# One distance between moving operand and weights: four operand buffers of a split-precision decoder trunk, on one Trainium2 core

## The chip, the cores and the metric

The kernel is one program on one core of a Trainium2 chip. The metric is its device time in microseconds (us), the median of several runs. Five engines are named as in the profile: PE (TensorE, with its weight loads as PEld), DVE (VectorE), ACT (ScalarE), POOL (GpSimd) and SP (SyncE, which issues most of the transfers).

## The reference

One decoder layer on 16 meta tokens and 256 tokens of width 2048, all in float32. What matters here is its chain of products:

```
xn   = rmsnorm(h)
proj = xn @ w_in                                  # attention and linear-attention inputs, gates
y    = sigmoid(gate_fox) * (o_fox @ w_o_fox) + sigmoid(gate_gla) * (o_gla @ w_o_gla)
h    = h + y @ w_out
h    = h + square(relu(rmsnorm(h) @ w_ff1)) @ w_ff2       # 2048 -> 8192 -> 2048
out  = rmsnorm(h)[:, 16:]
```

The heads of the two token mixers lie between `proj` and `y`; the change does not touch them.

## The kernel before, in words

Activations are kept transposed: 128 channels of a block on the 128 partitions, tokens along the free dimension. A matrix of 2048 columns of input is therefore 16 blocks, numbered k, and one *weight chunk* is a 2048 x 128 piece of a weight matrix: 16 blocks of 128 x 128. The order of the chunks is a list (`stream`), and the products follow it.

Each float32 factor is split in two: an upper part *hi*, rounded to the format in which PE takes it in one pass, and a lower part *lo*, the rest. A weight chunk arrives by two transfers of 512 KB on SP's queue (line 122); ACT writes hi (line 124) and DVE writes lo = raw - hi (line 125), side by side in one of five weight buffers `wt`, in half chunks of 8 blocks: hi of a block is 512 bytes per partition, lo of the same block the 512 bytes behind it. A product leaves out lo times lo. So `gemm2` (line 143) runs 16 *pairs* per chunk, with a moving operand of 256 tokens whose row k holds its own hi and lo next to each other:

```
        nc.tensor.matmul(ps, hi, x, start=first, stop=False)                          # L140: 512 columns
        nc.tensor.matmul(ps[:, 0:NT], lo, x[:, 0, :], start=False, stop=last)         # L141: 256 columns
```

A *row* of an operand is thus 2 x 256 numbers of 4 bytes, 2048 bytes per partition. The operands of `gemm2`:

- `x` (normalised input, rows of 272 tokens, so 2176 bytes) and `of` (attention output, 8 rows): not touched by the change.
- `og` (output of linear attention) and `x2` (normalised input of the MLP) share one buffer, "s2". The profile leaves buffer numbers out, so `x2` is printed as `x` there.
- `y` (input of `w_out`) and `a` (output of the first MLP matrix, a group of 2048 of the 8192 channels at a time, so four times) share another buffer, "s1".

`operand` (line 225) takes a tile of S1 or S2 numbers and cuts the 16 rows out of it at places given as a list. Before, `steps` (line 236) gives row k the place first + 512 k + (0, 64, 128 or 192) numbers for the four quarters of the rows: rows 2048 bytes apart, and 256 bytes more at every fourth. `first` is another one for each operand (lines 239 to 242).

From the token mixers on, the chunks run so: 8 rounds of four gate chunks on `x`, one on `of` (two halves of 8 pairs) and two on `og` (16 chunks of `og` in all); 16 chunks on `y` (line 789 and behind: each result is added to `h`, and `x2`'s row is made of it); then four times 16 chunks on `x2` followed by 16 chunks on `a`. In the last group only 12 chunks of `a` run as pairs; the last four keep their upper weights (`whi_last`, in buffer "s2") and run lo for all tokens first (line 850), then hi for 128 tokens at a time (line 859), so that the end can be normalised and stored in halves. In the MLP every product of the first matrix goes through `relu2` (lines 815 to 820), and every product of the second through `add_residual` (lines 774 to 777), on ACT and DVE. The instructions of an engine are put in order by a scheduler when the program is built.

Of the kernel before, what the change touches and what calls it, by code (L numbers as in the profile page):

```python
# [18 lines left out]
KT = D // P  # L19
NM = 16  # L20
NT = 256
# [44 lines left out]
def trunk(ctx: ExitStack, tc: tile.TileContext, hT, w_small, w_all, consts, w_alpha2, out):  # L66
# [3 lines left out]
    def nm(s):  # L70
        serial[0] += 1
        return f"{s}_{serial[0]}"

    const = ctx.enter_context(tc.tile_pool(name="const", bufs=1))
    keep = ctx.enter_context(tc.tile_pool(name="keep", bufs=1))
# [53 lines left out]
    def next_weights(keep_hi=None):  # L129
        c = chunk[0]  # L130
        chunk[0] += 1
        parts = []
        for i in range(2):
            hi, lo, step = weight_half(c, i, None if keep_hi is None else keep_hi[:, HK * i : HK * (i + 1), :])
            step(0, HK)
            parts.append((hi, lo))
        return lambda k: (parts[k // HK][0][:, k % HK, :], parts[k // HK][1][:, k % HK, :])
# [5 lines left out]
    def gemm2(w, x, k0=0, nk=KT):  # L143

        ps = bank(pg, "ps")
        for k in range(nk):
            hi, lo = w(k0 + k)
            mac2(ps, hi, lo, x[k], k == 0, k == nk - 1)
        issued()
        return ps  # L150
# [74 lines left out]
    def operand(pool, name, size, places, tag):  # L225


        t = pool.tile([P, size], F32R, tag=tag, name=nm(name))
        rows = []
        for at, gap in places:  # L230
            both = t[:, at : at + 2 * gap].rearrange("p (o t) -> p o t", t=gap) if at + 2 * gap <= size else None
            rows.append(both[:, :, 0:NT])
        return rows

    S1, S2 = 8728, 8628
    def steps(first, *by):
        return [(first + 512 * k + by[k * len(by) // KT], NT) for k in range(KT)]

    AT_OG = steps(8, 0, 64, 128, 192)
    AT_Y = steps(48, 0, 64, 128, 192)  # L240
    AT_X2 = steps(40, 0, 64, 128, 192)
    AT_A = [steps(e, 0, 64, 128, 192) for e in (16, 40, 12, 58)]


    h = keep.tile([P, KT, NA + 3], F32, name="h")
# [23 lines left out]
    def gain(i, k):  # L269
        return h[:, k, NA + i : NA + i + 1]  # L270
# [55 lines left out]
    for s in range(KT // 2):  # L326
# [3 lines left out]
        for kk in range(2):  # L330
            k = 2 * s + kk
# [100 lines left out]
    og_box = []  # L432

    def og_tile():
        if not og_box:
            og_box.append(operand(keep, "og", S2, AT_OG, "s2"))
        return og_box[0]

    def gla_gates(ts):
# [20 lines left out]
    def gla_head(hd, sg, ready=None):  # L460
# [122 lines left out]
        def scale():  # L583
            pr = st["pr"]
            spread(pr, st["y"], (0, P), NT)
            nc.scalar.copy(rg, pr[:, 0:NT])
            for i in range(4):
                j = 4 * hd + i
                nc.vector.scalar_tensor_tensor(oT[:, i, :], oT[:, i, :], ggn[:, j : j + 1], rg, op0=ALU.mult,
                                               op1=ALU.mult)  # L590
                nc.vector.tensor_tensor(oT[:, i, :], oT[:, i, :], st["sg"][:, i, :], op=ALU.mult)
                split_to(og_tile()[j][:, 0, :], og_tile()[j][:, 1, :], oT[:, i, :])
# [34 lines left out]
    for hd in range(1, GLA_H):  # L627
        gla_head(hd, None)
    flush()
    og = og_tile()  # L630


# [112 lines left out]
    for j0 in range(0, KT, 2):  # L745
# [5 lines left out]
        for j in range(2):  # L751
            t = total(gemm2(next_weights(), og))
            nc.vector.tensor_tensor(t, gates[2 * j + 1], t, op=ALU.mult)
            nc.vector.tensor_tensor(yf[:, j0 + j, :], gates[2 * j], t, op=ALU.add)
    y = operand(keep, "y", S1, AT_Y, "s1")
    for j in range(KT):
        split_to(y[j][:, 0, :], y[j][:, 1, :], yf[:, j, :])
    mix.close()
# [1 line left out]


    ht = h[:, :, NM:NA]
    x2 = operand(keep, "x2", S2, AT_X2, "s2")

    def square_sum(j, acc):
        if j == 0:
            nc.scalar.activation(acc, ht[:, j, :], AF.Square)
        else:
            sq = gat.tile([P, NT], F32, tag="hsq", name=nm("hsq"))
            nc.scalar.activation(sq, ht[:, j, :], AF.Square)  # L770
            nc.gpsimd.tensor_tensor(acc, acc, sq, op=ALU.add)

    def add_residual(j, ps):
        b = tmp.tile([P, NT], F32, tag="evb", name=nm("evb"))
        nc.scalar.copy(b, ps[:, NT:512])  # L775
        nc.vector.tensor_tensor(ht[:, j, :], ps[:, 0:NT], ht[:, j, :], op=ALU.add)
        nc.vector.tensor_tensor(ht[:, j, :], ht[:, j, :], b, op=ALU.add)
# [37 lines left out]
    def relu2(a, f, ps):  # L815
        t = total(ps)
        nc.vector.scalar_tensor_tensor(t, t, 0.0, r2b, op0=ALU.max, op1=ALU.mult)
        s = gat.tile([P, NT], F32, tag="asq", name=nm("asq"))
        nc.vector.tensor_tensor(s, t, t, op=ALU.mult)
        split_to(a[f][:, 0, :], a[f][:, 1, :], s)  # L820

    acc = gat.tile([P, NT], F32, tag="acc", name="acc3", bufs=1)
    for g in range(NG):
        a = operand(keep, "a", S1, AT_A[g], "s1")
        held = []
        for f in range(KT):
            ps = gemm2(next_weights(), x2)
            if g == 0 and f == 0:
                held.append(ps)
                continue  # L830
            if g == 0 and f == 1:
                relu2(a, 0, held.pop())
            relu2(a, f, ps)
        last = g == NG - 1
        for j in range(KT - NL if last else KT):
            add_residual(j, gemm2(next_weights(), a))
            if last:
                square_sum(j, acc)
                nc.scalar.activation(ht[:, j, :], ht[:, j, :], AF.Identity, scale=gain(2, j))
                if j == 0:  # L840
                    tc.keep_in_program_order(nc.scalar.preload_act_table_set("sqrt_and_others"))
# [121 lines left out]
```

## Time and profile before

| what | value |
|---|---|
| device time, median of 3 runs | 1631.77 us (1631.02 to 1631.82) |
| profiled execution, its own time | 1631.39 us |
| profiled execution, its span (first to last instruction) | 1629.7 us |
| PE busy | 1612.4 us, 99% |
| DVE, ACT, POOL busy | 1048.0, 793.7, 91.2 us |
| granted PE clock, mean | 0.996 |
| DMA | 292.97 MB, mean 180 GB/s |

The span lies within the profiled execution's own time, 1.7 us short of it. PE's busy time includes the overlap of matmuls in its pipeline: how long a matmul really takes of PE is read from the start of one to the start of the next, not from its listed duration.

### The profile page before, as it was taken

Reading aid. Unit: us, or ns where it says so; the run is one execution under the profiler, and the core shown is the slowest. Engines: PE = TensorE matmul, PEld = TensorE weight load, DVE = VectorE, ACT = ScalarE, POOL = GpSimd, SP = SyncE. Lnnn points to the kernel's source line nnn. Section 1 sums busy time; section 2 is a strip of 40 time slices with the busy share of each in tenths; the row PEclk is TensorE's granted clock in tenths of the full one; section 3 lists DMA queues with packets and bytes.
Section 4 is the critical chain, followed back from the end, with each engine's and each line's share of the span. In section 5 each row is a group of like instructions: output and inputs, shape, how many; then the busy total and the mean of one; then the engine's idle time right before and its main releaser. Section 6 shows DMA issues by size and latency. Waiting matters only on the chain.

```text
span 1629.7 us, 25555 instructions
## 1 busy us (share of the span) xinstructions
PE 1612.4 (99%) x9996; PEld 1450.3 (89%) x9996; DVE 1048.0 (64%) x1591; ACT 793.7 (49%) x1217; POOL 91.2 (6%) x144
## 2 busy tenths in 40 slices
PE   8999999999999999999999999999999999999997
PEld 7999999999998888888888888888888888888886
DVE  6766757476556566665677776567656776667655
ACT  6555444454445444444565444444444444444563
POOL 0100000010000000000011000000000000000012
PEclk9999999999999999999999999999999999999998
DMA  8444555454455555555555555555555555555552
GB/s 290 156 143 156 165 161 165 157 195 157 157 161 173 184 191 190 187 191 189 188 189 189 183 190 182 190 186 190 178 197 193 184 188 188 191 184 190 185 193 66
DMA packets 90265, 292.97 MB, mean 180 GB/s; under 512 B 9096, under 2 KB 21648, under 8 KB 89888
## 3 DMA queue, kind: packets, MB, share of 16 engines
q1 hardware_dynamic: 87552, 288.88, 54.1%
q8 instruction: 79, 1.29, 0.3%
q10 hardware_dynamic: 2416, 1.33, 0.3%
q0 software_dynamic: 176, 1.12, 0.2%
q14 instruction: 42, 0.34, 0.1%
HBM read 289.19 MB, written 2.11 MB: 179 GB/s over the span
## 4 chain that ended last, share of the span: by engine, by line
PE 98%; DMA 1%; DVE 0%; ACT 0%; issue 0%; SPq 0%; DVEq 0%; ACTq 0%
PE ps L140 50%; PE ps L141 26%; PE psa L159 5%; PE psa L158 5%; PE psa L157 5%; PE ps L345 1%; PE ps L859 1%; DMA h<-hT_dram 1%; PE pa L506 1%; PE ps L850 0%; PE ps L352 0%; PE po L570 0%; DMA raw<-w_all_dram 0%; PE pz L404 0%; ACT x L332 0%; PE po L571 0%
## 5 line engine op out<-in xcount | busy, mean ns | idle before, releaser
L125 DVE TENSOR_TENSOR wt<-raw,wt 128x1024 fp32r<-128x1024 f32 x522 | 644.7, 1235 | 330.0 <-ACT wt L124 320.0
L124 ACT CAST wt<-raw 128x1024 fp32r<-128x1024 f32 x522 | 548.7, 1052 | 397.3 <-issue 158.6
L140 PE MATMUL ps<-x,wt 128*128 128x512 f32 x1952 | 688.4, 395 | 0.0
L141 PE MATMUL ps<-x,wt 128*128 128x256 f32 x1952 | 551.3, 282 | 0.0
L140 PEld LDWEIGHTS ps<-x,wt 128*128 128x128 f32 x1952 | 366.8, 188 | 83.1
L141 PEld LDWEIGHTS ps<-x,wt 128*128 128x128 f32 x1952 | 367.9, 188 | 0.0
L140 PE MATMUL ps<-a,wt 128*128 128x512 f32 x960 | 336.8, 394 | 0.0
L141 PE MATMUL ps<-a,wt 128*128 128x256 f32 x960 | 270.8, 282 | 0.0
L140 PEld LDWEIGHTS ps<-a,wt 128*128 128x128 f32 x960 | 180.7, 188 | 41.0
L157 PE MATMUL psa<-x,wt 128*128 128x272 f32 x640 | 187.3, 293 | 0.0
L159 PE MATMUL psa<-x,wt 128*128 128x272 f32 x640 | 184.8, 289 | 0.0
L158 PE MATMUL psa<-x,wt 128*128 128x272 f32 x640 | 184.4, 288 | 0.0
L141 PEld LDWEIGHTS ps<-a,wt 128*128 128x128 f32 x960 | 181.5, 189 | 0.0
L166 ACT COPY evb<-ps 128x256 f32<-128x256 f32 x160 | 59.3, 373 | 237.6 <-PE ps L141 235.4
L169 DVE TENSOR_TENSOR evt<-ps,evb 128x256 f32<-128x256 f32 x158 | 66.9, 424 | 107.1 <-ACT evb L166 106.9
L157 PEld LDWEIGHTS psa<-x,wt 128*128 128x128 f32 x640 | 120.3, 188 | 0.7
L158 PEld LDWEIGHTS psa<-x,wt 128*128 128x128 f32 x640 | 120.4, 188 | 0.2
L159 PEld LDWEIGHTS psa<-x,wt 128*128 128x128 f32 x640 | 120.4, 188 | 0.1
L140 PE MATMUL ps<-y,wt 128*128 128x512 f32 x256 | 89.4, 393 | 0.0
L140 PE MATMUL ps<-og,wt 128*128 128x512 f32 x256 | 89.1, 394 | 0.0
L775 ACT COPY evb<-ps 128x256 f32<-128x256 f32 x76 | 28.3, 372 | 113.0 <-PE ps L141 112.9
L141 PE MATMUL ps<-y,wt 128*128 128x256 f32 x256 | 71.7, 280 | 0.0
(261 smaller groups left out, 1396.1 us busy)
## 6 DMA issues: line engine op xcount, KB each, us to landing
raw<-w_all_dram SPq DMA_DIRECT2D x537, 512.0 KB, 3.9
raw<-w_all_dram SPq DMA_DIRECT2D x7, 384.0 KB, 6.8
h<-hT_dram SPq DMA_DIRECT2D x1, 1100.0 KB, 10.0
negc<-fdram POOLq DMA_DIRECT2D x1, 1088.0 KB, 6.0
out_dram<-h SPq DMA_DIRECT2D x3, 256.0 KB, 2.6
out_dram<-h ACTq DMA_DIRECT2D x3, 256.0 KB, 3.1
h<-hT_dram SPq DMA_DIRECT2D x1, 550.0 KB, 7.3
raw<-w_all_dram SPq DMA_DIRECT2D x2, 256.0 KB, 4.4
```

Of the source, the lines that this page charges most:

```text
L124: nc.scalar.copy(hi[:, k, :], r)
L125: nc.vector.tensor_tensor(lo[:, k, :], r, hi[:, k, :].bitcast(F32), op=ALU.subtract)
L140: nc.tensor.matmul(ps, hi, x, start=first, stop=False)
L141: nc.tensor.matmul(ps[:, 0:NT], lo, x[:, 0, :], start=False, stop=last)
L157: nc.tensor.matmul(ps[:, 0:n], hi, x[:, k, 0, :], start=(k == 0), stop=False)
L158: nc.tensor.matmul(ps[:, 0:n], lo, x[:, k, 0, :], start=False, stop=False)
L159: nc.tensor.matmul(ps[:, 0:n], hi, x[:, k, 1, :], start=False, stop=(k == KT - 1))
L166: nc.scalar.copy(b, ps[:, NT:512])
L169: nc.vector.tensor_tensor(t, ps[:, 0:NT], b, op=ALU.add)
L345: nc.tensor.matmul(ps, hi, x[:, k, :, NM:NA], start=st, stop=False)
L506: nc.tensor.matmul(dst, k[:, a, :], q[:, a, :], start=(a == 0), stop=(a == 1))
L775: nc.scalar.copy(b, ps[:, NT:512])
```

## The change

Every row of `og`, `y`, `x2` and `a` is put at the same place modulo 256 bytes, and the extra 256 bytes at each fourth row go: rows are exactly 2048 bytes apart. Buffer "s2" becomes 384 numbers (1536 bytes) shorter.

```
-    S1, S2 = 8728, 8628
-    def steps(first, *by):
-        return [(first + 512 * k + by[k * len(by) // KT], NT) for k in range(KT)]
-
-    AT_OG = steps(8, 0, 64, 128, 192)
-    AT_Y = steps(48, 0, 64, 128, 192)
-    AT_X2 = steps(40, 0, 64, 128, 192)
-    AT_A = [steps(e, 0, 64, 128, 192) for e in (16, 40, 12, 58)]
+    S1, S2 = 8728, 8244
+    AT_S1 = [(40 + 512 * k, NT) for k in range(KT)]
+    AT_S2 = [(16 + 512 * k, NT) for k in range(KT)]
...
-            og_box.append(operand(keep, "og", S2, AT_OG, "s2"))
+            og_box.append(operand(keep, "og", S2, AT_S2, "s2"))
...
-    y = operand(keep, "y", S1, AT_Y, "s1")
+    y = operand(keep, "y", S1, AT_S1, "s1")
...
-    x2 = operand(keep, "x2", S2, AT_X2, "s2")
+    x2 = operand(keep, "x2", S2, AT_S2, "s2")
...
-        a = operand(keep, "a", S1, AT_A[g], "s1")
+        a = operand(keep, "a", S1, AT_S1, "s1")
```

The addresses that the built programs give (bytes from a partition's start): "s1" begins at 36928 and "s2" at 71840 in both. The five weight buffers begin at 127936 and every 8192 behind it before, and at 126400 and every 8192 behind it after: all that lies behind "s2" moves down by 1536 bytes, a multiple of 512. So hi and lo of every block begin at 192 modulo 256 in both programs. The table gives the *distance*: where a row of the operand begins, minus where its weights begin, modulo 256 bytes.

| operand | pairs | distance before | distance after |
|---|---|---|---|
| `x` | 928 | 192 and 64 in turn | the same |
| `of` | 128 | 0 | the same |
| `og` | 256 | 0 | 32 |
| `y` | 256 | 64 | 32 |
| `x2` | 1024 | 128 | 32 |
| `a`, group 0 | 256 | 192 | 32 |
| `a`, group 1 | 256 | 32 | 32 |
| `a`, group 2 | 256 | 176 | 32 |
| `a`, group 3 | 192 | 104 | 32 |
| `a`, last four chunks, line 850 (lo) | 64 matmuls | 104 | 32 |
| `a`, last four chunks, line 859 (hi) | 128 matmuls | 136 | 64 |

No instruction is added, removed or changed in shape, and on each of the five engines' queues the instructions stand in the same order in both programs. Line numbers behind the edit are 5 lower in the changed kernel.

## The prediction

> **What bounds the kernel now.** I read the page's busy times and its chain first, to see whether PE's pairs set the end, and then the timeline of PE alone, to see what a pair costs with each operand.
>
> ```profile
> PE 1612.4 (99%) x9996; PEld 1450.3 (89%) x9996; DVE 1048.0 (64%) x1591; ACT 793.7 (49%) x1217; POOL 91.2 (6%) x144
> ...
> PE 98%; DMA 1%; DVE 0%; ACT 0%; issue 0%; SPq 0%; DVEq 0%; ACTq 0%
> PE ps L140 50%; PE ps L141 26%; PE psa L159 5%; PE psa L158 5%; PE psa L157 5%; PE ps L345 1%; PE ps L859 1%; DMA h<-hT_dram 1%; PE pa L506 1%; PE ps L850 0%; PE ps L352 0%; PE po L570 0%; DMA raw<-w_all_dram 0%; PE pz L404 0%; ACT x L332 0%; PE po L571 0%
> ...
> L140 PE MATMUL ps<-a,wt 128*128 128x512 f32 x960 | 336.8, 394 | 0.0
> L141 PE MATMUL ps<-a,wt 128*128 128x256 f32 x960 | 270.8, 282 | 0.0
> ```
>
> The chain that ended last is PE for 98% of the span, and the two lines of the pair are 76% of it: what a pair gains or loses, the end gains or loses. The two groups under it show why the page cannot tell the cost: 394 + 282 = 676 ns of listed time for one pair, while the next pair starts after about half of that. So I take starts. Below is the timeline of PE (start, duration, line, operation), cut to the first matmul of each stage: `of`, `og`, the `x` behind it, `y`, and then `x2` (printed as x) and `a` in turn, four times, up to the first matmul of the last four chunks.
>
> ```profile
> 516.01 0.39 PE L140 MATMUL ps<-of,wt 128*128 128x512 f32 x1
> 521.56 0.39 PE L140 MATMUL ps<-og,wt 128*128 128x512 f32 x1
> 532.65 0.39 PE L140 MATMUL ps<-x,wt 128*128 128x512 f32 x1
> 805.93 0.40 PE L140 MATMUL ps<-y,wt 128*128 128x512 f32 x1
> 895.26 0.39 PE L140 MATMUL ps<-x,wt 128*128 128x512 f32 x1
> 985.99 0.39 PE L140 MATMUL ps<-a,wt 128*128 128x512 f32 x1
> 1076.44 0.39 PE L140 MATMUL ps<-x,wt 128*128 128x512 f32 x1
> 1166.32 0.40 PE L140 MATMUL ps<-a,wt 128*128 128x512 f32 x1
> 1255.09 0.40 PE L140 MATMUL ps<-x,wt 128*128 128x512 f32 x1
> 1344.97 0.39 PE L140 MATMUL ps<-a,wt 128*128 128x512 f32 x1
> 1434.56 0.39 PE L140 MATMUL ps<-x,wt 128*128 128x512 f32 x1
> 1524.43 0.40 PE L140 MATMUL ps<-a,wt 128*128 128x512 f32 x1
> 1592.28 5.92 PE L850 MATMUL ps<-a,wt 128*128 128x256 f32 x48
> ```
>
> Differences of neighbouring starts give the time of a stage, and its number of pairs the time of a pair. Distances are those of the table ahead.
>
> - `og`, 32 pairs at distance 0: 532.65 - 521.56 = 11.09 us, 346.6 ns a pair. `of`, 16 pairs at 0: 5.55 us, 346.9 ns.
> - `y`, 256 pairs at 64: 89.33 us, 348.9 ns.
> - `x2`, 256 pairs at 128 each time: 90.73, 89.88, 89.88, 89.87 us; the last three are 351.1 ns a pair. The first has 0.85 us more, at its start.
> - `a`, 256 pairs: 90.45 us at 192 (353.3 ns), 88.77 us at 32 (346.8 ns), 89.59 us at 176 (350.0 ns); then 192 pairs at 104 in 67.85 us (353.4 ns).
>
> The same two instructions cost between 346.6 and 353.4 ns, and what differs between the four visits to `a` is above all the place of the rows. Group 1 of `a` already stands exactly where the change puts every row, at 224 modulo 256 bytes against weights at 192: its 88.77 us are the row for everything that follows.
>
> **The change part by part.** It adds and removes no instruction, so every term is a number of pairs by a difference of two rows, and all of it lies on PE's chain.
>
> First, the distance of 32 bytes. `y`: 89.33 - 88.77 = 0.56 us less. `x2`: 1.11 us less at each of the first three visits and 1.10 at the last, 4.43 in all (the extra 0.85 us of the first visit I leave standing). `a`: 90.45 - 88.77 = 1.68, nothing for group 1, 89.59 - 88.77 = 0.82, and for group 3 67.85 - 192 x 0.34676 = 1.27. `og`: 346.6 against 346.8 ns, which is nothing to within 0.1 us over 256 pairs. The sum is 0.56 + 4.43 + 1.68 + 0.82 + 1.27 = 8.76 us.
>
> Second, the rows without the extra 256 bytes at each fourth. Nothing in `a` shows such a tile as a whole, but its quarters do: rows 0, 4, 8 and 12 of one chunk of group 1 begin the four quarters, which lie at 0, 256, 512 and 768 bytes of shift against the weights.
>
> ```profile
> 1199.62 0.39 PE L140 MATMUL ps<-a,wt 128*128 128x512 f32 x1
> ...
> 1201.01 0.39 PE L140 MATMUL ps<-a,wt 128*128 128x512 f32 x1
> ...
> 1202.39 0.39 PE L140 MATMUL ps<-a,wt 128*128 128x512 f32 x1
> ...
> 1203.78 0.39 PE L140 MATMUL ps<-a,wt 128*128 128x512 f32 x1
> ...
> 1205.17 0.39 PE L140 MATMUL ps<-a,wt 128*128 128x512 f32 x1
> ```
>
> The four quarters take 1.39, 1.38, 1.39 and 1.39 us: a shift by a multiple of 256 bytes costs nothing that shows. `of` has packed rows of 2048 bytes without extra steps and costs 346.9 ns where `og`, with the steps, costs 346.6 at the same distance. So I take nothing, with bounds of 0.3 ns a pair either way, 0.75 us over the 2496 pairs. The same rows cover the 1536 bytes by which all later buffers move, a multiple of 512, which leaves every distance modulo 256 of `x` and `of` as it was.
>
> Third, the last four chunks, single matmuls of 256 columns: 48 begin with the last row of the timeline above, and these follow.
>
> ```profile
> 1598.05 1.86 PE L859 MATMUL ps<-a,whi_last 128*128 128x256 f32 x14
> ...
> 1601.98 8.57 PE L859 MATMUL ps<-a,whi_last 128*128 128x256 f32 x70
> 1610.39 0.28 PE L877 MATMUL pn<-ones,acc 128*128 128x1 f32 x2
> ```
>
> They take 5.77 / 48 = 120.2 and 8.41 / 70 = 120.1 ns. No row shows them at their new distances. A pair at 104 costs 353.4 - 346.8 = 6.6 ns more than at 32; a third of that for a third of the columns is 2.2 ns, 0.14 us over the 64 of line 850. For line 859, from 136 to 64, the nearest rows are `x2` at 128 and `y` at 64: 2.2 ns a pair, 0.7 ns a matmul, 0.09 us over 128. I take 0.23 us less; the bounds are 2.2 ns either way on all 192, 0.42 us less to 0.42 us more.
>
> What must keep up if PE runs faster is the splitting of weights on ACT and DVE and the transfers. The window table shows busy time of each engine in the stages `a` group 0, `x2` second visit, `a` group 1:
>
> ```profile
> core 0: us, PE busy (x) PEld busy (x) DVE busy (x) ACT busy (x) POOL busy (x), PEclk, DMA share, GB/s
> 985.99:1076.44 90.45, 90.45 (x515) 78.59 (x513) 53.14 (x67) 38.27 (x49) 0.00 (x0) 1.00 0.57 187
> 1076.44:1166.32 89.88, 89.88 (x514) 78.78 (x513) 62.81 (x94) 42.51 (x63) 0.00 (x0) 1.00 0.57 187
> 1166.32:1255.09 88.77, 88.77 (x515) 78.68 (x514) 53.13 (x67) 38.24 (x49) 0.00 (x0) 1.00 0.58 191
> ```
>
> DVE is the nearest: 62.81 us in an `x2` visit, which would be 71% of 88.77 us. The DMA engines stand at 58% in the stage that already runs at the new pace. So the faster PE finds its weights, and if that cover failed it would cost at most what is won.
>
> PE's gain is then 8.76 + 0.23 = 8.99 us. The profiled execution took 1631.39 us, so its like would take 1622.4, with a span of 1620.7; the median of the runs lies 0.38 us above the profiled one, so I forecast 1622.8 us.
>
> A page of the Trainium skill speaks against all of this. TensorE: Matmul & The Clock Gate, section Part 2 (What happens when you issue a matmul), says that PE reads moving operand and weights through two independent ports and that "Loading the next tile's weights doesn't steal SBUF read bandwidth from the running matmul." By that rule the place of a row would not matter, and the sum would be 0 in place of 8.99 us. This trace does not agree with it as far as it goes: 353.3 and 346.8 ns for the same pair in groups 0 and 1 of `a`.
>
> **The rivals.** *The place is not the cause.* If the pair's time hung on when a stage runs or on what DVE, ACT and the transfers do beside it, moving the rows would change nothing: 1631.8 us. For it speaks only that each place was seen in its own stage. Against it: groups 0 and 1 of `a` have the same load beside them (DVE 53.14 and 53.13 us, ACT 38.27 and 38.24) and differ by 1.68 us, while `x2`, with DVE busier at 62.81 us, is faster than group 0, and its last three visits, spread over 450 us of the run, agree to 0.01 us. The skill's two-port rule above would lead here too. Chance 0.03.
>
> *Half of it.* `x2` lies in the other buffer, and no row shows 32 bytes there; if something of its own (DVE's load, or that buffer) holds it at 351.1 ns, its 4.43 us are not won: 1627.2 us. Against it: `og` in the same buffer runs at 346.6. Chance 0.06.
>
> *Packed rows cost.* The extra 256 bytes spread the rows over four distances modulo 1024; without them all 16 rows of a chunk stand at the same one. If a clash over longer strides then lasted for a whole chunk, each pair might cost what the worst place costs, 353.4 ns: `og` 1.74, `y` 1.14, `x2` 2.37, `a` 0.02 + 1.70 + 0.88 us more, 7.85 in all, 1639.6 us. It decides from the mean of the 2496 pairs now: 88.7 (256 x 346.6 ns) + 89.33 + 359.51 (90.73 without its 0.85, 89.88, 89.88, 89.87) + 336.66 us (the four of `a`) are 874.2 us, 350.2 ns a pair; if packed rows cost more than that, the change is slower. Against it stand the equal quarters and `of`. Chance 0.03.
>
> **How the numbers follow.** The forecast's case has the remaining 0.88. Its own bounds: 0.1 us for `og`, 0.75 for the packing, 0.42 about zero for the last chunks, and the runs' spread of 0.75 below and 0.05 above the median. They do not fall on one side together, so I take about 1.2 us below and, since half-way cases lie only above, 2.2 us above: 1621.6 to 1625.0, which leaves out the rivals and some of the forecast's own edge. A measurement of this kernel can tell about 0.2%, 3.3 us, from no change. Faster by more than that are the forecast and the half case (4.6 us), 0.94; within it the first rival, 0.03; slower the last, 0.03.
>
> **What would show it.** In the profile after, every visit to `y`, `x2` and `a` should last 88.8 us (66.6 for the last one, 0.85 more for the first `x2`), pairs of `og` should stay at 346.6 ns and those of `x` and `of` as they are. If `x2` stays at 89.88 us the half case holds; if `og` and group 1 of `a`, which had the best places, become slower than 347 ns, packing costs; if groups 0 to 3 of `a` still differ from one another, the place was not the cause and the prediction is wrong.

## The result, and the profile after

| | before | after |
|---|---|---|
| median of 6 runs, side by side | 1631.24 us (1630.65 to 1631.82) | 1622.38 us (1621.21 to 1623.53) |
| profiled execution, its own time | 1631.39 us | 1622.43 us |
| its span | 1629.7 us | 1620.7 us |
| granted PE clock, mean | 0.996 | 0.996 |

The ratio of the times is 0.9946 (95% interval 0.9933 to 0.9959): faster by 0.5%, where 0.2% can be told from no change. The forecast was 1622.8 us (1621.6 to 1625.0). Of all executions told of below, one of experiment 2 took 6013 us where the other three took 1621 to 1623 us; the record does not show why, and it is left out.

The page of the changed kernel has the same chain: PE is still 98% of it. Its busy time is 9.0 us less, with the same number of instructions; the other engines have the busy time that they had.

```profile
PE 1603.4 (99%) x9996; PEld 1450.2 (89%) x9996; DVE 1048.7 (65%) x1591; ACT 793.7 (49%) x1217; POOL 91.4 (6%) x144
...
PE 98%; DMA 1%; DVE 0%; ACT 0%; issue 0%; SPq 0%; DVEq 0%; ACTq 0%
```

The timeline of PE in the changed kernel, cut at the same places as that of before (start, duration, line, operation; `of`, `og`, `x`, `y`, then `x2`, printed as x, and `a` in turn, and the last four chunks, whose lines are now 845 and 854):

```profile
516.47 0.39 PE L140 MATMUL ps<-of,wt 128*128 128x512 f32 x1
522.02 0.39 PE L140 MATMUL ps<-og,wt 128*128 128x512 f32 x1
533.13 0.40 PE L140 MATMUL ps<-x,wt 128*128 128x512 f32 x1
806.50 0.39 PE L140 MATMUL ps<-y,wt 128*128 128x512 f32 x1
895.25 0.39 PE L140 MATMUL ps<-x,wt 128*128 128x512 f32 x1
984.87 0.39 PE L140 MATMUL ps<-a,wt 128*128 128x512 f32 x1
1073.62 0.39 PE L140 MATMUL ps<-x,wt 128*128 128x512 f32 x1
1162.37 0.39 PE L140 MATMUL ps<-a,wt 128*128 128x512 f32 x1
1251.11 0.39 PE L140 MATMUL ps<-x,wt 128*128 128x512 f32 x1
1339.86 0.39 PE L140 MATMUL ps<-a,wt 128*128 128x512 f32 x1
1428.61 0.39 PE L140 MATMUL ps<-x,wt 128*128 128x512 f32 x1
1517.35 0.39 PE L140 MATMUL ps<-a,wt 128*128 128x512 f32 x1
1583.91 5.76 PE L845 MATMUL ps<-a,wt 128*128 128x256 f32 x48
1589.51 1.81 PE L854 MATMUL ps<-a,whi_last 128*128 128x256 f32 x14
...
1593.30 8.41 PE L854 MATMUL ps<-a,whi_last 128*128 128x256 f32 x70
1601.54 0.28 PE L872 MATMUL pn<-ones,acc 128*128 128x1 f32 x2
...
1606.94 0.38 PE L223 MATMUL pn<-diag,ones 128*128 128x128 f32 x2
```

The row of line 872 begins the closing norm; 42 of the 192 single matmuls run between it and the last row. Before, that last row stood here:

```profile
1615.88 0.38 PE L223 MATMUL pn<-diag,ones 128*128 128x128 f32 x2
```

Every visit to `y`, `x2` and `a` is now 88.74 to 88.75 us long, 346.7 ns a pair; only the first of `x2` is longer, 89.62, as it was before. The four groups of `a`, which differed by up to 1.7 us, are alike. From here on a visit of 256 pairs is told as its time or as ns a pair, whichever is shorter (88.75 us are 346.7 ns a pair).

The same rows account for all of it. Between the first `of` and the first matmul of the closing norm (line 877 before, 872 after), before took 1610.39 - 516.01 = 1094.38 us and after 1601.54 - 516.47 = 1085.07, which is 9.31 less. Of these `y` gave 0.58, `x2` 4.50, `a` 3.86 (1.70, 0.03, 0.84 and 1.29) and the 150 single matmuls that lie ahead of the norm 0.48; `og` and the `x` behind it took back 0.11. The span became 9.0 us shorter, not 9.3, because `of` began 0.46 us later and the end, from the norm's first matmul on, took 0.1 us less (0.09 of it in the other 42 single matmuls).

### The profile page after: what moved, and what is told of

It is laid out like the page before. It is cut to its first block, busy times and chain, and to the rows that moved or that the text cites. A ratio compares the mean times of both kernels' runs of the same rounds, so it can differ in the third digit from the quotient of the medians.

```text
span 1620.7 us, 25555 instructions
## 1 busy us (share of the span) xinstructions
PE 1603.4 (99%) x9996; PEld 1450.2 (89%) x9996; DVE 1048.7 (65%) x1591; ACT 793.7 (49%) x1217; POOL 91.4 (6%) x144
## 3 DMA queue, kind: packets, MB, share of 16 engines
q8 instruction: 79, 1.29, 0.3%
## 4 chain that ended last, share of the span: by engine, by line
PE 98%; DMA 1%; DVE 0%; ACT 0%; issue 0%; SPq 0%; DVEq 0%; ACTq 0%
PE ps L140 50%; PE ps L141 26%; PE psa L159 5%; PE psa L158 5%; PE psa L157 5%; PE ps L340 1%; PE ps L854 1%; DMA h<-hT_dram 1%; PE pa L501 1%; PE ps L347 0%; PE ps L845 0%; PE po L565 0%; DMA raw<-w_all_dram 0%; PE pz L399 0%; ACT x L327 0%; PE po L566 0%
## 5 line engine op out<-in xcount | busy, mean ns | idle before, releaser
L140 PE MATMUL ps<-a,wt 128*128 128x512 f32 x960 | 333.0, 390 | 0.0
```

## The experiments

Three readings of the gain were to be told apart: by the distance between row and weights, by the place of the row alone, and by the packing of the rows. Each diff is against the changed kernel. In the first four kernels either the weights, or rows and weights, or the packing, or the first places alone differ. The times of stages are read from one profiled execution of each kernel.

**1. Only the weights move, by 128 bytes** (every row at distance 160 instead of 32):

```
-    S1, S2 = 8728, 8244
+    S1, S2 = 8728, 8276
```

> The changed kernel with buffer s2 made 128 bytes longer: rows of og, y, x2 and a stay where the change put them, at 224 modulo 256, while all weight buffers (and what lies behind them) move by 128 bytes, so the distance between rows and weights becomes 160. Theory A, the distance to the weights modulo 256 sets the pair's time: a pair of these four operands goes from 346.7 ns to between 350.0 (the row of group 2 of a at 176 before) and 351.1 ns (x2 at 128 before), which over 2496 pairs is 8.2 to 11.0 us, so a span of 1629 to 1632 us; the pairs of x merely swap their two distances and stay at 350.0 ns, of stays at 0 and 346.4 ns. Theory B, the place of the row itself modulo 256 sets it, whatever the weights do: all four operands stay at 346.7 ns and the span at 1620.7 us; of, which moves, would change. Theory C, the packing without steps brought the gain: also no change.

Measured: 1622.66 us, ratio to before 0.9947 (0.9933 to 0.9962), span 1621.7 us. The timeline of its PE, at the first `of` and `og` and around one visit to `x2`:

```profile
516.61 0.39 PE L140 MATMUL ps<-of,wt 128*128 128x512 f32 x1
522.26 0.40 PE L140 MATMUL ps<-og,wt 128*128 128x512 f32 x1
...
1074.56 0.39 PE L140 MATMUL ps<-x,wt 128*128 128x512 f32 x1
...
1163.31 0.39 PE L140 MATMUL ps<-a,wt 128*128 128x512 f32 x1
```

The visit takes 88.75 us, and so do the others: distance 160 is as good as 32. The price for it that had been interpolated between the known distances, 350 to 351 ns, fell: the cost is no smooth function of the distance. One operand became slower, `of`, which still lies at distance 0, since it moves with the weights: 5.65 us for its 16 pairs against 5.55, 353 ns in place of 347. Over its 128 pairs that is some 0.8 us, most of the 1.0 us by which the span is longer than that of the changed kernel. This slower `of` at an unchanged distance comes back below.

**2. Rows and weights move together, by 128 bytes** (distance 32 again, rows at 96 and weights at 64 instead of 224 and 192):

```
-    S1, S2 = 8728, 8244
-    AT_S1 = [(40 + 512 * k, NT) for k in range(KT)]
-    AT_S2 = [(16 + 512 * k, NT) for k in range(KT)]
+    S1, S2 = 8728, 8276
+    AT_S1 = [(72 + 512 * k, NT) for k in range(KT)]
+    AT_S2 = [(48 + 512 * k, NT) for k in range(KT)]
```

> The same with the rows of og, y, x2 and a moved by the same 128 bytes: distance 32 again, rows at 96 and weights at 64 modulo 256. Theory A: 346.7 ns a pair everywhere and a span of 1620.7 us, as in the changed kernel. Theory B: another place of the rows, so another time; 96 has not been seen, its neighbours before, 112 (group 2 of a) and 64 (x2), cost 350.0 and 351.1 ns, which gives 1629 to 1632 us. Theory C: 1620.7 us.

Measured: 1622.09 us (median of three), ratio 0.9946 (0.9926 to 0.9966), all visits 88.75 us. `of`, at distance 0 as always, takes 5.64 us here too. By itself this only shows that the pair of places 224 and 192 is nothing special; with experiments 5 and 6 it becomes evidence for the distance.

**3. The extra 256 bytes at each fourth row come back, the first places stay**:

```
-    S1, S2 = 8728, 8244
-    AT_S1 = [(40 + 512 * k, NT) for k in range(KT)]
-    AT_S2 = [(16 + 512 * k, NT) for k in range(KT)]
+    S1, S2 = 8728, 8436
+    AT_S1 = [(40 + 512 * k + 64 * (k // 4), NT) for k in range(KT)]
+    AT_S2 = [(16 + 512 * k + 64 * (k // 4), NT) for k in range(KT)]
```

> The changed kernel with the extra 256 bytes at every fourth row put back, the distance left at 32 modulo 256 everywhere. Theory A: 346.7 ns a pair and 1620.7 us of span, since 256 bytes more leave the distance alone. Theory C, the packing does it: back to the pair times of before and 1629.7 us.

Measured: 1622.08 us, ratio 0.9943 (0.9929 to 0.9958), all visits 88.75 us: the same as the changed kernel.

**4. Rows packed, but at the first places of before** (each operand takes its own list, as in all kernels below that name several):

```
+    AT_Y = [(48 + 512 * k, NT) for k in range(KT)]
+    AT_A = [[(e + 512 * k, NT) for k in range(KT)] for e in (16, 40, 12, 58)]
+    AT_OG = [(8 + 512 * k, NT) for k in range(KT)]
+    AT_X2 = [(40 + 512 * k, NT) for k in range(KT)]
```

> The changed kernel with the first places of before (og 0, y 64, x2 128, a 192, 32, 176 and 104 bytes from the weights) and rows packed without steps. Theory A: each operand at its time of before, og 346.6, y 348.9, x2 351.1, a 353.3, 346.7, 350.0 and 353.4 ns a pair, and a span of 1629.7 us. Theory C: 346.7 ns for all and 1620.7 us.

Measured: 1631.58 us, ratio 1.000 (0.9991 to 1.001). The timeline of its PE at the ends of `a` group 0 and of the second visit to `x2`:

```profile
985.74 0.39 PE L140 MATMUL ps<-a,wt 128*128 128x512 f32 x1
...
1076.19 0.39 PE L140 MATMUL ps<-x,wt 128*128 128x512 f32 x1
...
1166.08 0.40 PE L140 MATMUL ps<-a,wt 128*128 128x512 f32 x1
```

Group 0 takes 90.45 us and `x2` 89.89, what they took before to 0.01 us. Experiments 3 and 4 halve the change: the first places do all of it, the packing nothing.

**5. The rows at other places, weights as they were (192)**. Distances: `og` 80, `y` 16, `x2` 224, `a` 96, 224, 160 and 48:

```
+    def packed(first):
+        return [(first + 512 * k, NT) for k in range(KT)]
+
+    AT_OG, AT_Y, AT_X2 = packed(28), packed(36), packed(0)
+    AT_A = [packed(e) for e in (56, 24, 8, 44)]
```

> The changed kernel (packed rows, weights at 192 modulo 256) with another place for each operand: rows of og at 16, y at 208, x2 at 160 and the four groups of a at 32, 160, 96 and 240 modulo 256, so at distances of 80, 16, 224, 96, 224, 160 and 48 bytes. Theory A, the distance modulo 256, has fallen in its first form (160 cost what 32 does). Theory A2, the distance modulo 128 must be 32: only group 2 of a (160) runs at 346.7 ns a pair, groups 0 and 1 and x2 are slower, 350 to 353 ns. Theory D, a row must begin at 32 modulo 64, whatever the weights do: groups 0, 1 and 2 of a and x2 all at 346.7 ns. Theory E, row and weights must lie 32 apart modulo 64: the same three groups and x2, since the weights are at 0 modulo 64 here. Rows at 16 or 48 modulo 64 (og, y, group 3): by the one row seen, 350.0 ns at 48 modulo 64; no theory says.

Measured: 1635.85 us, ratio 1.0025 (1.0014 to 1.0035): slower than before. The timeline of its PE from `y` on:

```profile
806.97 0.40 PE L140 MATMUL ps<-y,wt 128*128 128x512 f32 x1
899.14 0.40 PE L140 MATMUL ps<-x,wt 128*128 128x512 f32 x1
990.27 0.40 PE L140 MATMUL ps<-a,wt 128*128 128x512 f32 x1
1079.88 0.40 PE L140 MATMUL ps<-x,wt 128*128 128x512 f32 x1
1170.32 0.40 PE L140 MATMUL ps<-a,wt 128*128 128x512 f32 x1
1260.77 0.40 PE L140 MATMUL ps<-x,wt 128*128 128x512 f32 x1
1351.23 0.39 PE L140 MATMUL ps<-a,wt 128*128 128x512 f32 x1
1439.97 0.39 PE L140 MATMUL ps<-x,wt 128*128 128x512 f32 x1
```

`y` at 16 takes 92.17 us, 360.0 ns a pair, the most seen anywhere; yet 16 bytes to either side, at 0 and at 32, a pair takes 346.7. The three groups of `a` in these rows take 89.61 (at 96), 90.45 (at 224) and 88.74 us (at 160, which confirms experiment 1 with other absolute places). Group 3 at 48 runs at 346.7 ns. Each of the readings expected above missed part of this. That the row's own place modulo 64 decides is out: the rows at distances 96 and 224 begin at 32 and 160 bytes, just like the good ones 32 above a multiple of 64, and are slow.

**6. Weights at 224, rows at six distances**: `og` 32, `y` 0, `x2` 0, `a` 32, 64, 128 and 192. The diff is that of experiment 5 with these numbers:

```
+    S1, S2 = 8728, 8252
+    AT_OG, AT_Y, AT_X2 = packed(24), packed(40), packed(16)
+    AT_A = [packed(e) for e in (48, 56, 8, 24)]
```

> The changed kernel with s2 made 32 bytes longer, so that all weights lie at 224 modulo 256, 32 modulo 64; rows of og at 0, y at 224, x2 at 224 and the groups of a at 0, 32, 96 and 160, so at distances of 32, 0, 0, 32, 64, 128 and 192. Theory D, rows at 32 modulo 64: y, x2 and groups 1, 2 and 3 of a at 346.7 ns a pair, og and group 0 of a slower, up to 353 ns. Theory E, 32 apart modulo 64: og and group 0 of a at 346.7 ns, and the others by their distance as before: y and x2 346.6 (0), groups 1, 2 and 3 348.9 (64), 351.1 (128) and 353.3 ns (192). Theory A2, 32 apart modulo 128: as E.

Measured: 1630.64 us, ratio 0.9995 (0.9985 to 1.0005). Its timeline from the first group of `a` on:

```profile
986.35 0.40 PE L140 MATMUL ps<-a,wt 128*128 128x512 f32 x1
1075.10 0.39 PE L140 MATMUL ps<-x,wt 128*128 128x512 f32 x1
1163.85 0.40 PE L140 MATMUL ps<-a,wt 128*128 128x512 f32 x1
1254.31 0.39 PE L140 MATMUL ps<-x,wt 128*128 128x512 f32 x1
1343.06 0.39 PE L140 MATMUL ps<-a,wt 128*128 128x512 f32 x1
1432.93 0.40 PE L140 MATMUL ps<-x,wt 128*128 128x512 f32 x1
1523.38 0.39 PE L140 MATMUL ps<-a,wt 128*128 128x512 f32 x1
```

Group 0, at distance 32 with rows at 0 modulo 256, takes 88.75 us; at 128 (1343.06 to 1432.93) it is 89.87, what `x2` took at 128 before; at 192 it was 353.2 ns, as for group 0 of before. So the distances keep their times when both absolute places change, which speaks for the distance once more. But two rows speak against a table of distances. Distance 64 takes 90.46 us, 353.3 ns, where `y` took 348.9 at 64 before. And `x2`, the same tile read by the same instructions at distance 0, takes 88.75 us twice and then, behind group 2 of `a`, 90.45: one kernel, one address, two rates, each held for 256 pairs. By the starts in the trace the fast pairs take 346 or 347 ns, while the slow ones repeat every three pairs: 349, 350 and 361 ns. What ran before a stage is the one difference found between these visits, then.

**7. `x` moved by 96 bytes too**, to 32 and 160 in turn:

```
-    x = keep.tile([P, KT, 2, NA], F32R, tag="s1", name="x")
+    x = keep.tile([P, S1], F32R, tag="s1", name="x")[:, 24:].rearrange("p (k o t) -> p k o t", o=2, t=NA)
```

> The changed kernel with x moved by 96 bytes within its buffer, so that its rows for the pairs begin at 224 and 96 modulo 256 in turn (distances 32 and 160) instead of 128 and 0, and its rows for the triples of lines 157 to 159 at 160 and 32 (hi) and 224 and 96 (lo) instead of 64, 192, 128 and 0. Theories D, E and A2: the 928 pairs of x fall from 350.0 to 346.7 ns, 3.1 us; by D and E the 640 triples gain too, by no row so far, and at most the 10 ns by which a triple lies over another now; so a span of 1611 to 1618 us. A theory in which only packed rows can gain (x has rows of 2176 bytes): no change, 1620.7 us.

Measured: 1623.08 us, ratio 0.9947 (0.9933 to 0.9960): no gain over the changed kernel. Its timeline over one round:

```profile
515.97 0.39 PE L140 MATMUL ps<-of,wt 128*128 128x512 f32 x1
521.61 0.40 PE L140 MATMUL ps<-og,wt 128*128 128x512 f32 x1
532.71 0.39 PE L140 MATMUL ps<-x,wt 128*128 128x512 f32 x1
555.11 0.39 PE L140 MATMUL ps<-of,wt 128*128 128x512 f32 x1
```

The 64 pairs of `x` take 22.40 us, 350.0 ns, exactly as at 192 and 64, though 32 and 160 were the two best distances. And `of`, whose rows and weights haven't moved at all, needs 5.64 us in place of 5.55. Only the operand ahead of it differs: the second case of a rate that depends on what ran before. It was so in experiments 1 and 2 as well, where moving the weights left `of` at 0 but made `x`, which runs ahead of it, lie at 64 and 192 in turn in place of 192 and 64. And in experiment 6, where the weights at 224 put the untouched `x` at 160 and 32 in turn, its 64 pairs took 22.61 us, 353.3 ns: the two distances of this experiment, begun with the other one, at another rate. Two questions follow: does the turn from row to row cost, or do the rows of `x`, whose halves lie 1088 and not 1024 bytes apart (it skips 16 meta tokens), count by both halves?

**8. Rows whose distance changes in turn.** `y` and group 0 of `a` 32 and 160, group 1 32 and 64, group 2 0 and 128, group 3 192 and 64. Rows overlap by up to 128 bytes here, so a piece of lo in such a row is overwritten by the row behind it:

```
+    def turns(even, odd):
+        return [((odd if k % 2 else even) + 512 * k, NT) for k in range(KT)]
+
+    AT_OG, AT_X2 = turns(16, 16), turns(16, 16)
+    AT_Y = turns(40, 72)
+    AT_A = [turns(40, 72), turns(40, 48), turns(32, 64), turns(80, 48)]
```

> The changed kernel with rows that change their distance from row to row: y and group 0 of a at 32 and 160 in turn (each alone cost 346.7 ns), group 1 of a at 32 and 64, group 2 at 0 and 128, group 3 at 192 and 64; og and x2 stay at 32. Theory H, each pair costs what its own distance costs: y and group 0 346.7 ns, group 1 348 to 350, group 2 348.9, group 3 351.1 ns. Theory G, PE falls into a rhythm that a constant distance keeps and a change from row to row breaks: y and group 0 near the 351.1 ns that x showed at 32 and 160 in turn, and group 3 at the 350.0 ns of x before. A theory in which x is slow for its rows of 2176 bytes sides with H here.

Measured: 1625.0 us (one run), span 1623.3. Its timeline from `y` to the end of group 0 of `a`:

```profile
806.36 0.39 PE L140 MATMUL ps<-y,wt 128*128 128x512 f32 x1
895.95 0.40 PE L140 MATMUL ps<-x,wt 128*128 128x512 f32 x1
985.58 0.39 PE L140 MATMUL ps<-a,wt 128*128 128x512 f32 x1
1075.16 0.40 PE L140 MATMUL ps<-x,wt 128*128 128x512 f32 x1
```

`y` and group 0 take 89.58 to 89.59 us, 349.9 ns a pair, although each distance by itself takes 346.7: a time that belongs to each pair alone would give 346.7, so it is out. Group 1 (32 and 64) runs at 346.7, group 2 at 348.3, group 3 at 350.0. Only `y` and group 0 are dearer than the mean of their two distances alone. The other three groups are cheaper than theirs: 346.7 against at least 347.8, 348.3 against at least 348.9, 350.0 against at least 351.1 ns. (The expectation's 351.1 ns for `x` at 32 and 160 in turn is not what experiment 7 showed, 350.0.)

**9 and 10. lo of the weights moved apart from hi.** Each weight buffer gets a block of hi and, 4096 bytes on, a block of lo; in the second kernel lo begins 96 bytes further:

```
-        return wp.tile([P, HK, 2, P], F32R, tag="wt", name=nm("wt"))
+        t = wp.tile([P, 2 * HK * P + 64], F32R, tag="wt", name=nm("wt"))
+        return [t[:, at : at + HK * P].rearrange("p (k m) -> p k m", m=P) for at in (0, HK * P + 24)]
...
+    AT_OG, AT_Y, AT_X2 = packed(40), packed(64), packed(16)
+    AT_A = [packed(e) for e in (40, 64, 32, 8)]
```

The first has `HK * P + 0` there, and every row at distance 32.

> The changed kernel with the weight buffers laid out anew: the upper weights of 8 blocks together, the lower weights of the 8 blocks behind them, 4096 bytes on, both at 192 modulo 256 as before. A control for the next run: all theories 346.7 ns for og, y, x2 and a, and 1620.7 us.

Measured: 1622.34 us (one run), all visits 88.75 us. The other order of the blocks changes nothing.

> The same layout with the lower weights moved 96 bytes on, to 32 modulo 256, so that a row has two distances, one to hi and one to lo: x2 and group 0 of a 32 and 192; y, og and group 1 of a 128 and 32; group 2 0 and 160; group 3 160 and 64. Theory F1, the load of lo, which runs under the matmul of 512 columns, sets the cost: x2 and group 0 near 353.3 ns, y, og, group 1 and group 2 at 346.7, group 3 at 349 to 353. Theory F2, the load of hi, which runs under the matmul of 256 columns: x2, group 0, group 2 and group 3 at 346.7, y, og and group 1 at 351.1. If both count, only group 2 keeps 346.7 ns.

Measured: 1624.84 us (one run). Its timeline around group 2 of `a` (the line is 141 in this kernel):

```profile
1251.98 0.39 PE L141 MATMUL ps<-x,wt 128*128 128x512 f32 x1
1340.73 0.40 PE L141 MATMUL ps<-a,wt 128*128 128x512 f32 x1
1430.76 0.39 PE L141 MATMUL ps<-x,wt 128*128 128x512 f32 x1
```

With two distances, to hi and to lo: `x2` and group 0 at 32 and 192 take 88.75 us, `y`, `og` and group 1 at 128 and 32 346.7 to 346.8 ns a pair. One load of weights at 32 is enough, whichever of the two it is, though 192 and 128 alone cost 353.3 and 351.1. Group 2 at 0 and 160, both good alone, takes 90.03 us, 351.7 ns, and group 3 at 160 and 64 348.3. None of the three expectations had this. Nor is 351.7 ns the price of 0 and 160 as such: `of` lies at these two distances in this kernel too and keeps 5.55 us for its 16 pairs, 346.9 ns.

**11. `x` with rows 2304 bytes apart**, so that its hi halves all lie at 160, as do the rows of every other operand (weights at 224):

```
-    S1, S2 = 8728, 8244
-    AT_S1 = [(40 + 512 * k, NT) for k in range(KT)]
+    S1, S2 = 9184, 8216
+    AT_S1 = [(16 + 512 * k, NT) for k in range(KT)]
...
+    xs = keep.tile([P, S1 + 32], F32R, tag="s1", name="x")
+    x = xs.rearrange("p (k e) -> p k e", e=576)[:, :, 0 : 2 * NA].rearrange("p k (o t) -> p k o t", t=NA)
...
-        s = late.tile([P, NT], F32, tag="gate", name=nm("gate"), bufs=6)
+        s = late.tile([P, NT], F32, tag="gate", name=nm("gate"), bufs=5)
```

> The changed kernel with rows of x 2304 bytes apart in place of 2176, so that x too has one distance in all rows; buffer s1 grows, the gate buffers go from six to five to make room, and og, y, x2, a and x all lie at 160 (of stays at 0). Theory G: x falls from 350.0 to 346.7 ns a pair, 3.1 us over 928 pairs, the others stay at 346.7 ns; the triples of x, at 96 (hi) and 160 (lo), have no row, and I allow 2 us either way; a span of 1616 to 1620 us. Theory H: x at 160 also 346.7 ns, the same. If x is slow for another reason: 1620.7 us.

Measured: 1623.64 us, ratio 0.9952 (0.9938 to 0.9965); span 1622.5, 1.8 us longer than that of the changed kernel. From the timeline of PE, `x` of one round:

```profile
532.63 0.39 PE L140 MATMUL ps<-x,wt 128*128 128x512 f32 x1
555.25 0.40 PE L140 MATMUL ps<-of,wt 128*128 128x512 f32 x1
```

22.62 us for 64 pairs, 353.4 ns, with no turning left, while `y`, `x2` and `a` at the same 160 run at 346.7 and `og` at 347.3. (The rows of `a` begin at 128 modulo 256 here, just where group 0 began before, at 353.3 ns with the weights elsewhere: the place of the row by itself does not set the rate.) What is left to tell them apart is the second half of the row, which in `x` lies at 160 + 1088, that is at 224.

**12. That second half in `a`.** Rows 2304 apart in `y`, `a` and `x`; in `a` lo lies 1088 bytes behind hi, as in `x`. Distances of the two halves: group 0 160 and 224, group 1 192 and 0, group 2 96 and 160, group 3 224 and 32; both halves of `y` at 32:

```
-    S1, S2 = 8728, 8244
-    AT_S1 = [(40 + 512 * k, NT) for k in range(KT)]
+    S1, S2 = 9216, 8216
+    def wide(first, gap):
+        return [(first + 576 * k, gap) for k in range(KT)]
+
+    AT_Y = wide(48, NT)
+    AT_A = [wide(e, NA) for e in (16, 24, 0, 32)]
```

(`x` and the gate buffers as in experiment 11.)

> The kernel of x_one_distance, with rows of y and a 2304 bytes apart too, and in a with the lo half of a row 1088 bytes behind its hi half, as in x, so that the two halves of a 512-column matmul lie at two distances: group 0 of a at 160 and 224, group 1 at 192 and 0, group 2 at 96 and 160, group 3 at 224 and 32; y, with halves 1024 bytes apart, at 32; x as it was, at 160 and 224. Theory J, both halves count: group 0 repeats the 353.3 ns of x in x_one_distance, where operands with both halves at 160 cost 346.7. Theory K, the start of the row alone counts and x is slow for another reason: group 0 346.7, group 1 353.3, group 2 350.0, group 3 353.3 ns. By both theories y stays at 346.7 ns, with rows 2304 bytes apart.

Measured: 1628.39 us (one run), span 1626.6. Its timeline from group 0 of `a` to the end of group 1:

```profile
986.60 0.39 PE L140 MATMUL ps<-a,wt 128*128 128x512 f32 x1
1077.05 0.39 PE L140 MATMUL ps<-x,wt 128*128 128x512 f32 x1
1165.79 0.39 PE L140 MATMUL ps<-a,wt 128*128 128x512 f32 x1
1254.55 0.39 PE L140 MATMUL ps<-x,wt 128*128 128x512 f32 x1
```

Group 0 takes 90.45 us, 353.3 ns, what `x` takes at the same two halves in experiment 11, where `a` with both halves at 160 took 88.75, behind the same `x2` at 160. `y`, with rows 2304 apart and both halves at 32, keeps 88.75. So it is the lo half, not the spacing of the rows, and both halves of the moving operand count. It can go the other way as well: group 1 with halves at 192 and 0 takes 88.76 us, where both at 192 took 90.45 before (behind `x2` at 128, though, and here behind `x2` at 160). Group 2 runs at 350.0 ns, group 3 at 353.3.

Taken together, for operands with one distance to both loads and no turning, a pair of 768 columns took the following. Few orders of stages were tried, so a single figure is what was seen, not a fixed price.

| distance | ns a pair | distance | ns a pair |
|---|---|---|---|
| 0 | 346.7, or 352.6 to 353.3 behind some operands | 104 | 353.4 |
| 16 | 360.0 | 128 | 351.1 |
| 32 | 346.7 | 160 | 346.7 |
| 48 | 346.7 | 176 | 350.0 |
| 64 | 348.9 or 353.3 | 192 | 353.3 |
| 80, 96 | 350.0 | 224 | 353.3 |

## Why the prediction was right

*The reading of before.* That pairs set the end, and that starts, not durations, tell their price, held: 9.31 us less between the same two matmuls, 9.0 us less span, no other engine's busy time different by more than 0.7 us.

*Distance 32 everywhere.* The row on which the sum stood, group 1 of `a` with 88.77 us, carried over to three other operands and the other buffer: 88.74 to 88.75. The terms came out as 0.58 for 0.56 (`y`), 4.50 for 4.43 (`x2`) and 3.86 for 1.68 + 0.82 + 1.27 = 3.77 (`a`). The half case, in which `x2` keeps 351.1 ns for a reason of its own, didn't occur.

*The packing at nothing.* Right, and the bound of 0.75 us wasn't needed: with steps and without them all visits agree to 0.01 us (experiments 3 and 4). The rival of 1639.6 us had no effect behind it.

*`og`.* Taken as nothing to within 0.1 us; the 32 pairs of the rows above take 11.11 in place of 11.09 us, and by the starts in the trace all 256 take 88.85 in place of 88.74. That is a small loss, as large as the bound: the rate that settles is 346.7, and the first pairs behind `of` are slower.

*The last four chunks.* This term was mis-sized: 0.23 us forecast for the 192 matmuls, 0.57 measured from their first start to the row of line 223 behind them (23.60 us before, 23.03 after), past the bound of 0.42. The estimate scaled the differences of pairs to single matmuls by columns. It put 2.2 ns on line 850 and 0.7 on 859; the first 48 of the one take 116.7 ns now in place of 120.2, the run of 70 of the other 117.7 in place of 120.1.

*The total.* 8.99 us forecast, 8.96 between the profiled times. So close an agreement is partly luck: the stages gave 9.31, and a start 0.46 us later took some of that back.

*"The place is not the cause"* is refuted: experiment 4 has the changed kernel's packing at the old places and is as slow as before, experiment 3 the old steps at the new places and is as fast as after.

*What the prediction didn't say.* It treated a pair's time as a function of one distance. For the change this was enough, since 32 kept its rate behind every operand that ran ahead of it here. As a general rule it fails: the rate at 0 and 64 isn't single-valued (6, 7), turning rows change it (8), and so do the distances to lo (10) and of the second half (12). What can be said is that the rate belongs to the repeating sequence of reads, hi and lo loads and both halves, and to how a stage is entered. Which reads collide in the hardware, and how, stays open: the loads of weights were never taken out, so it isn't shown that they are the other side. One other candidate, the writing of the weight buffers by ACT and DVE, can be put aside. In group 0 of `a` before, DVE wrote weights during at least 95% of 95 pairs, ACT during at least 95% of 64, and neither wrote at all during 21; the three kinds took 353.3, 353.3 and 353.4 ns a pair. The rule of two independent ports in the Trainium skill (TensorE: Matmul & The Clock Gate, Part 2), by which the sum would have been 0, does not give what these runs show: moving nothing but rows in experiment 5 takes a pair from 346.7 to 360.0 ns.

No kernel tried beats the changed one by more than the interval. One lead wasn't tried: `x` with rows 2304 bytes apart and halves at 192 and 0, which ran at 346.7 ns in group 1 of experiment 12. If it did so for all 928 pairs of `x`, which take 350.0 now, that would be 928 x 3.3 ns = 3.1 us.

## What to carry to other kernels

Where one engine's repeated pair of instructions is nearly all of the chain, compare stages that issue the same instructions: the fastest one, measured from start to start, says what the others may gain, and whatever is set differently there (here an address) can be carried over as a whole. Carry over a place that a trace has shown, and measure any other: between two distances at 346.7 ns lay one at 360.0, and the interpolated price of 160 was wrong by 4 ns. When splitting such a change, test each half by itself, as with the first places and the packing, before explaining either.

## What the runs showed of the hardware

- The address of a matmul's moving operand relative to its weights, modulo 256 bytes, changed a pair's time by up to 3.8% (346.7 to 360.0 ns for 768 columns), at a granted clock of 0.995 to 0.997.
- The same tile at the same address ran at two rates in one execution, 88.75 and 90.45 us a visit, each held from end to end (experiment 6); an operand that wasn't touched changed from 5.55 to 5.64 us because the one ahead of it had moved (7).
- Each half of a moving operand of 2 x 256 columns counts: 160 and 224 takes 353.3 ns, 192 and 0 346.7, where 160 alone takes 346.7 and 192 alone 353.3.
- Two distances that are good alone can be bad together: 0 to hi and 160 to lo took 351.7 ns in `a`, though 346.9 in `of` (10), and 32 and 160 in turn 349.9 (8).
- Whether ACT or DVE were writing weight buffers made no difference to a pair: 353.3 to 353.4 ns either way in group 0 of `a` before.
